# A hybrid decoder step on one core: TensorE in source order, gate and u products between the matmuls of S5 and attention

## The chip, the cores and the metric

The kernel runs on one core of one Trainium2 chip. The metric is the device time of one execution in microseconds. The kernel before takes 1735.41 us (median of 3 runs, 1729.68 to 1736.14).

## The reference

One layer of a hybrid decoder, for a prompt of 1024 tokens and for 8 sequences of 4 new tokens, of width 1024, all in float32:

```
proj = rmsnorm(x, norm1_g) @ w_in        # q, k, v (12 heads x 64), u (512), gate_a, gate_s (1024 each)
# branch A: for 3 dilation groups of 4 heads, causal dilated window attention with a bias by distance;
#           the groups of a head slot are merged by their softmax denominators -> 256 channels
# branch B: S5: 32 groups of 16 channels, each with a 64-wide complex diagonal state;
#           y = Re(C h) + D u, gelu, then y * sigmoid(y @ w_glu + b_glu)
mix = sigmoid(gate_a) * (attn_out @ w_branch_attn) + sigmoid(gate_s) * (ssm_out @ w_branch_ssm)
x   = x + mix @ w_out
a, val = split(rmsnorm(x, norm2_g) @ w_up)          # 2816 each
x   = x + (silu(causal_conv3(a)) * val) @ w_down    # then a final rmsnorm
```

It also returns the new key and value rows, the final S5 states and the convolution's last inputs. The samples attend to cached keys and values of up to 2048 positions.

## The kernel before, in words

All tokens form 1056 columns (4 residues of 256 prompt columns and 8 sample columns each); features lie on partitions. A matrix product is done in three fp32r passes (weights and activations each split into a high and a low part): `gemm` (L159) makes a tile of 128 outputs from 8 steps of k, each of 9 matmuls of 128x352. `load_w` (L145) fetches 128 columns of weights (two buffers), multiplies them by the norm's gain `g1c` where they meet x (L154), and splits them (L155, L156). Three PSUM banks hold one tile's result.

The work goes through stages:

- x is loaded, transposed and split raw (L226 to L243); 1/rms of each token is made beside it and spread over columns as `rb1`. Each product of x is multiplied by `rb1` when it leaves PSUM (L268 for u, L336 for gates, L732 for q, k, v), on VectorE.
- `u_tile` makes 4 tiles of u, which go to DRAM and come back in another layout as `U`. The bias table by distance is made by fp32 one-hot matmuls (L286).
- The parameters of S5 are worked out by a long chain of small operations on VectorE and POOL (L374 to L590), ending in the Toeplitz matrix `Mm`.
- The S5 loop (L605) takes 16 pairs of groups: two transpositions and two matmuls (L624), a rotation and scans on VectorE with one step on POOL (L631 to L644), copies of H on ScalarE (L646), three matmuls (L650 to L652) and a gelu.
- The attention takes 6 units (3 groups by 2 head pairs) of 8 blocks of queries. A block has logits (L839), the bias and row maxima on VectorE (L844), exp on ScalarE, transpositions to `pT`, a copy (L855) and the value product into `pO` (L858). Beside each block `cached` multiplies one sequence's cached keys by its queries on POOL (L817) and sums them on VectorE into `Lk` (L818). `proj` makes q, k, v of the next unit. `merge` combines the groups after each head pair; its weights are spread by transpositions of `lb` (L903).
- Then come the samples' attention (with V tiles loaded by POOL's queue, L967), the GLU and the projections of both branches, the output projection (L1102) and the channel mixer (L1147 on).

A planner orders every engine's instructions from its own estimate of their times, TensorE's too. `gates_after` binds 16 gate tiles to places named by `PLAN`: three after the S5 loop, six spread within it, two before units of the attention, and five after it. A gate tile gets its sigmoid (L337) and is stored in `sgd`.

Of the kernel before, what the change touches and what calls it, by code (L numbers as in the profile page):

```python
# [38 lines left out]
# columns of the one-hot matrix, group by group (dilation 1, 4, 16)  # L39
# [4 lines left out]
COFF = (R0W, R1W, R2W)                       # cached keys of the decode, in the group  # L44
SOFF = (R0W + 512, R1W + 128, R2W + 128)     # new keys of the decode, in the group
# [9 lines left out]
def _onehot():  # L55
    """[33, NCOLS]: column -> the bucket of its distance, or row 32 where the key is masked."""
# [26 lines left out]
    return (np.arange(33)[:, None] == idx[None]).astype(np.float32)  # L83
# [12 lines left out]
def body(tc, I, O):  # L96
# [12 lines left out]
    with root:  # L109
# [18 lines left out]
        rb1 = cst.tile([P, T], F32, name="rb1")  # L128
        prm = cst.tile([P, 2 * KD + 4], F32, name="prm")
        mult = cst.tile([P, 16], F32, name="mult")         # 0, 1, 2, ...  # L130
# [4 lines left out]
        cbf = cst.tile([P, NF, 16], F32, name="cbf")      # (i, b)  # L135
        g1c, g2c, bglu = prm[:, :KD], prm[:, KD:2 * KD], prm[:, 2 * KD:]

        nc.gpsimd.dma_start(g1c, I['norm1_g'][0].rearrange("(k p) -> p k", p=P), allow_slow_non_contiguous=True)
# [6 lines left out]
        def load_w(src, kt, g=None, mw=P, E1=V_, E2=V_):  # L145
            """mw columns of a weight matrix, [kt*128, mw] -> exact parts hi + lo, [128, kt, mw]."""
# [6 lines left out]
            if g is not None:  # L153
                E1.tensor_tensor(raw, raw, g[:, :kt, None].to_broadcast([P, kt, mw]), OP.mult)  # L154
# [4 lines left out]
        def gemm(ps, w, acts, m0=0, k0=0, by_chunk=False):  # L159
            """ps[c] += w^T act; acts: [(hi, lo)] by k."""  # L160
            hi, lo = w
            n = len(acts)
            if by_chunk:
                for c in range(NCH):
                    for k in range(n):
                        for j, (wt, xt) in enumerate(((lo, acts[k][0]), (hi, acts[k][1]), (hi, acts[k][0]))):
                            PE.matmul(ps[c][:, :CH], wt[:, k0 + k, m0:m0 + P], xt[:, cs(c)],
                                      start=k == 0 and j == 0, stop=k == n - 1 and j == 2)
                return
            for k in range(n):  # L170
# [4 lines left out]
                for c, j in runs:  # L175
                    wt, xt = ((lo, xh), (hi, xl), (hi, xh))[j]
                    PE.matmul(ps[c][:, :CH], wt[:, k0 + k, m0:m0 + P], xt[:, c * CH:(c + 1) * CH],  # L177
                              start=k == 0 and j == 0, stop=k == n - 1 and j == 2)

# [11 lines left out]
        xp_ = pool("xact", 1)  # L191
        xh = xp_.tile([P, KD, T], F32R, name="xh")
        xl = xp_.tile([P, KD, T], F32R, name="xl")
        X = [(xh[:, k], xl[:, k]) for k in range(KD)]
        xhv, xlv = (t.rearrange("p k (s c) -> p k s c", s=S4) for t in (xh, xl))

# [1 line left out]
        s2 = root.enter_context(ExitStack())  # L198
        sp = pool("s5", 1, stack=s2)

# [6 lines left out]
        st3 = xin.tile([P, 3, 9], F32, name="st3")  # L207
        st, rst, tmp12 = (st3[:, x] for x in range(3))
        G_.memset(st, 1.0)
# [11 lines left out]
        def x_tile(src, extra=False):  # L221
            t = go.tile([P, T], F32, name="go")[:, :D] if extra else xin.tile([P, D], F32, name="xt", bufs=4)
            nc.sync.dma_start(t[:src.shape[0]], src)
            return t[:src.shape[0]]

        xt0 = [x_tile(xpv[h][:, 0]) for h in range(2)]  # L226
        xs = x_tile(I['x_sample'].rearrange("b t d -> (b t) d"))
        for s in range(S4):
            xt = [x_tile(xpv[h][:, s], (s, h) in ((1, 1), (2, 0))) for h in range(2)] if s else xt0
            for k2 in range(0, KD, 2):  # L230
                pt = p3.tile([P, 512], F32, name="pt")
                for k in range(2):
                    for h in range(2):
                        tr(pt[:, (2 * k + h) * P:(2 * k + h + 1) * P], xt[h][:, (k2 + k) * P:(k2 + k + 1) * P])
                split(xhv[:, k2:k2 + 2, s, :256], xlv[:, k2:k2 + 2, s, :256], pt.rearrange("p (k c) -> p k c", k=2))
            if s == 0:
                pt = p3.tile([P, 512], F32, name="pt")
                for k in range(KD):
                    tr(pt[:, k * 32:(k + 1) * 32], xs[:, k * P:(k + 1) * P])
                split(xhv[:, :, :, 256:], xlv[:, :, :, 256:], pt[:, :256].rearrange("p (k b s) -> p k s b", k=KD, s=S4))  # L240
                A_.activation(xs, xs, AF.Square, accum_out=st[:32, 8:9])
            for h in range(2):
                A_.activation(xt[h], xt[h], AF.Square, accum_out=st[:, h * 4 + s:h * 4 + s + 1])  # L243
        rsqrt(rst, st, tmp12, V_)
        for s in range(S4):
            pt = p3.tile([P, 512], F32, name="pt")
            for h in range(2):
                tr(pt[:, h * P:(h + 1) * P], rst[:, h * 4 + s:h * 4 + s + 1].to_broadcast([P, P]))
            V_.tensor_copy(sc(rb1)[:, s, :256], pt[:, :256])
        pt = p3.tile([P, 512], F32, name="pt")  # L250
        tr(pt[:, :32], rst[:32, 8:9].to_broadcast([32, P]))
        V_.tensor_copy(sc(rb1)[:, :, 256:].rearrange("p s b -> p b s"), pt[:, :32].rearrange("p (b s) -> p b s", s=S4))
# [4 lines left out]
        sgd = dr.tile([2, D, T], F32, name="sgd")  # L257

# [1 line left out]
        udv = ud.rearrange("(i q) (s c) -> s q i c", q=32, s=S4)  # L260

        def u_tile(m):
            w = load_w(w_in[:, 2304 + m * P:2304 + (m + 1) * P], KD, g1c, E1=G_, E2=G_)
            ps = gbanks()
            gemm(ps, w, X, by_chunk=m == 0)
            uT = go.tile([P, T], F32, name="go")
            for c in range(NCH):
                V_.tensor_tensor(uT[:, cs(c)], ps[c][:, :CH], rb1[:, cs(c)], OP.mult)  # L268
            nc.sync.dma_start(ud[m * P:(m + 1) * P], uT)

        u_tile(0)

# [1 line left out]
        tab = xin.tile([33, 3, 32], F32, name="tab")  # L274
        G_.memset(tab, NEG)
        nc.gpsimd.dma_start(tab[:32, :, :4], I['rel_bias'].rearrange("b (g h) -> b g h", g=3))
        vec = dr.tile([4, NCOLS], F32, name="vec")
        blocks = [(g, a, min(512, GCOLS[g] - a)) for g in range(3) for a in range(0, GCOLS[g], 512)]
        for b0 in range(0, len(blocks), 4):
            pt = p3.tile([P, 512], F32, name="pt")  # L280
            for j, (g, a, n) in enumerate(blocks[b0:b0 + 4]):
                if j % 2 == 0:
                    oh2 = xin.tile([P, D], F32, name="xt", bufs=4)[:33]
                oh = oh2[:, j % 2 * 512:]
                nc.sync.dma_start(oh[:, :n], I['onehot'][:, GOFF[g] + a:GOFF[g] + a + n])
                PE.matmul(pt[32 * j:32 * j + 32, :n], tab[:, g], oh[:, :n], start=True, stop=True,  # L286
                          tile_position=(0, 32 * j))
# [1018 lines left out]
```

## Time and profile before

| what | value |
| --- | --- |
| median of 3 runs | 1735.41 us |
| profiled execution, span | 1739.8 us (no other time of it is shown) |
| busy PE / PEld / DVE / ACT / POOL | 95% / 89% / 50% / 28% / 27% of the span |
| instructions | 25386 |
| mean granted TensorE clock | 0.970 |
| bytes moved | 149.53 MB, mean 86 GB/s |

PE is TensorE's matmuls, PEld its weight loads, DVE VectorE, ACT ScalarE, POOL GpSimd, SP SyncE. PEclk is the granted TensorE clock, as a share of full speed. A busy PE includes matmuls that run at the low clock.

### The profile page before, as it was taken

How to read it: one execution, taken by the hardware profiler on the slowest of the kernel's cores; microseconds unless marked ns; L12 is line 12 of the kernel's file. 1: busy time of each engine (PE TensorE's matmuls, PEld its weight loads, DVE VectorE, ACT ScalarE, POOL GpSimd, SP SyncE). 2: the span in 40 equal slices, each digit the busy share in tenths (PEclk: the TensorE clock that was granted, in tenths of full speed). 3: DMA queues.
4: the chain of work that ended last, by engine and by line, in shares of the span. 5: the costliest groups of instructions: out<-in, count | busy, mean ns of one | idle time of the engine just before them, and what ended most of it. 6: DMA issues, size and time to landing. Idle time of an engine off the chain costs nothing.

```text
span 1739.8 us, 25386 instructions
## 1 busy us (share of the span) xinstructions
PE 1648.9 (95%) x10272; PEld 1554.8 (89%) x10272; DVE 865.4 (50%) x1472; ACT 495.2 (28%) x892; POOL 465.5 (27%) x498
## 2 busy tenths in 40 slices
PE   6978888988999999999999999999999999999997
PEld 5677778977888888979899999999999999999996
DVE  3598986344445544534763434434444344444445
ACT  5103333333433343421322222121121212111126
POOL 7474662022112202250672121020110201110114
PEclk9899999999999988999999999999999999999999
DMA  7341223254225413477711110211202111020122
GB/s 183 93 118 50 62 75 84 74 141 129 83 78 145 143 58 82 165 229 242 228 49 49 37 49 27 65 36 33 73 19 67 34 47 54 28 63 28 57 63 100
DMA packets 220094, 149.53 MB, mean 86 GB/s; under 512 B 30517, under 2 KB 208159, under 8 KB 219978
## 3 DMA queue, kind: packets, MB, share of 16 engines
q1 hardware_dynamic: 207002, 128.12, 25.3%
q10 hardware_dynamic: 10224, 10.36, 1.9%
q0 software_dynamic: 2752, 9.44, 1.6%
q8 instruction: 80, 1.31, 0.3%
q14 instruction: 36, 0.29, 0.1%
HBM read 122.03 MB, written 27.82 MB: 86 GB/s over the span
## 4 chain that ended last, share of the span: by engine, by line
PE 75%; DVE 10%; DMA 6%; issue 4%; POOL 3%; SPq 1%; ACT 1%; DVEq 0%; POOLq 0%; ACTq 0%
PE pg L177 68%; DMA qb<-qd 2%; DMA wraw<-in_w_in_dram 1%; PE pa L839 1%; DVE H L644 1%; PE pO L858 1%; PE pg L1250 1%; PE pT L142 1%; DVE mm L631 1%; PE pa L142 1%; POOL qb L817 1%; DVE wlo L156 1%; DVE wraw L154 1%; DVE mm L632 1%; DMA cache<-in_cache_kv_w_dram 1%
## 5 line engine op out<-in xcount | busy, mean ns | idle before, releaser
L177 PE MATMUL pg<-xh,wlo 128*128 128x352 f32 x1944 | 531.0, 332 | 24.5 <-DVE go L732 8.8
L177 PE MATMUL pg<-xl,whi 128*128 128x352 f32 x1944 | 526.7, 330 | 0.0
L177 PE MATMUL pg<-xh,whi 128*128 128x352 f32 x1944 | 526.2, 330 | 0.0
L177 PEld LDWEIGHTS pg<-xh,wlo 128*128 128x128 f32 x1944 | 354.0, 192 | 34.4 <-DVE go L732 9.9
L177 PEld LDWEIGHTS pg<-xl,whi 128*128 128x128 f32 x1944 | 355.0, 193 | 4.9 <-issue 3.9
L177 PEld LDWEIGHTS pg<-xh,whi 128*128 128x128 f32 x1944 | 354.2, 192 | 4.6 <-issue 3.5
L155 ACT CAST whi<-wraw 128x1024 fp32r<-128x1024 f32 (+2 forms) x156 | 132.9, 852 | 746.9 <-PE pg L177 478.2
L156 DVE TENSOR_TENSOR wlo<-wraw,whi 128x1024 fp32r<-128x1024 f32 (+2 forms) x152 | 158.0, 1039 | 65.2 <-ACT whi L155 63.4
L1153 POOL COPY ext<-ext 128x510 f32<-128x510 f32 x22 | 15.7, 712 | 524.5 <-DVE ext L1152 524.5
L177 PE MATMUL pg<-hh,wlo 128*128 128x352 f32 x480 | 148.0, 325 | 0.0
L177 PE MATMUL pg<-hl,whi 128*128 128x352 f32 x480 | 147.0, 322 | 0.0
L177 PE MATMUL pg<-hh,whi 128*128 128x352 f32 x480 | 146.6, 323 | 0.0
L817 POOL TENSOR_TENSOR qb<-kt,qb 128x512 f32<-128x512 f32 x48 | 62.1, 1304 | 277.6 <-DMA qb<-qd 219.9
L1180 DVE TENSOR_TENSOR y<-pg,y 128x352 f32<-128x352 f32 x168 | 84.6, 524 | 99.0 <-PE pg L177 98.3
L1152 DVE TENSOR_TENSOR ext<-pg,rb 128x352 f32<-128x352 f32 x66 | 32.7, 525 | 154.2 <-PE pg L177 154.2
L177 PEld LDWEIGHTS pg<-hh,wlo 128*128 128x128 f32 x480 | 88.9, 188 | 0.5
L177 PEld LDWEIGHTS pg<-hl,whi 128*128 128x128 f32 x480 | 89.2, 189 | 0.0
L177 PEld LDWEIGHTS pg<-hh,whi 128*128 128x128 f32 x480 | 88.7, 188 | 0.0
L1167 DVE TENSOR_TENSOR go<-pg,cv 128x352 f32<-128x352 f32 x66 | 31.2, 521 | 111.6 <-PE pg L177 111.6
L154 DVE TENSOR_TENSOR wraw<-wraw,prm 128x1024 f32<-128x1024 f32 x34 | 47.9, 1409 | 75.5 <-DMA wraw<-in_w_in_dram 75.5
L1161 POOL TENSOR_TENSOR cv<-cv,rb 128x1056 f32<-128x1056 f32 x22 | 54.3, 2469 | 55.0 <-ACT cv L1160 52.7
L818 DVE TENSOR_REDUCE Lk<-qb 128x8 f32<-128x512 f32 x48 | 33.0, 688 | 64.3 <-POOL qb L817 64.1
(585 smaller groups left out, 2301.7 us busy)
## 6 DMA issues: line engine op xcount, KB each, us to landing
wraw<-in_w_up_dram SPq DMA_DIRECT2D x44, 512.0 KB
wraw<-in_w_in_dram SPq DMA_DIRECT2D x38, 512.0 KB
qb<-qd SPq DMA_DIRECT2D x48, 256.0 KB
wraw<-in_w_down_dram SPq DMA_DIRECT2D x48, 192.0 KB
sgd<-go SPq DMA_DIRECT2D x16, 528.0 KB
kt<-in_cache_kv_w_dram SPq DMA_DIRECT2D x32, 256.0 KB
cache<-in_cache_kv_w_dram POOLq DMA_DIRECT2D x16, 512.0 KB, 5.7
go<-sgd SPq DMA_DIRECT2D x8, 528.0 KB
```

The source lines that it names most:

```text
L142: PE.transpose(out, in_, ident[:n, :n])
L154: E1.tensor_tensor(raw, raw, g[:, :kt, None].to_broadcast([P, kt, mw]), OP.mult)
L155: A_.copy(hi, raw)
L156: E2.tensor_tensor(lo, raw, hi.bitcast(F32), OP.subtract)
L177: PE.matmul(ps[c][:, :CH], wt[:, k0 + k, m0:m0 + P], xt[:, c * CH:(c + 1) * CH], start=k == 0 and j == 0, stop=k == n - 1 and j == 2)
L631: V_.tensor_tensor(m[x], ps[x][:, None, :256].to_broadcast([P, 2, 256]), rt, OP.mult)
L817: G_.tensor_tensor(qb, kv_, qb, OP.mult)
L818: V_.tensor_reduce(Lk[:, g, pr * 64:pr * 64 + 64].rearrange("p (h r) -> p h r", h=2)[:, :, 4 * b:4 * b + 4] .rearrange("p h t -> p t h"), ...
L1152: V_.tensor_tensor(ef[:, 2 * C + c * CH:2 * C + (c + 1) * CH], ps[c][:, :CH], rb2[:, cs(c)], OP.mult)
L1161: G_.tensor_tensor(cv, cv, rb2, OP.mult)
L1167: V_.tensor_tensor(t[:, cs(c)], ps[c][:, :CH], cv[:, cs(c)], OP.mult)
L1180: V_.tensor_tensor(y[m][:, cs(c)], ps[c][:, :CH], y[m][:, cs(c)], OP.add)
```

## The change

TensorE's instructions are taken in the order of the source up to the second merge, while the other engines stay with the planner. Products with `w_in` become jobs; `fill(n)` sets n steps of k of the next job at the place where it is called. Calls stand in the S5 preparation, in the S5 loop (8 gate tiles, 4 before it) and between the parts of every attention block (15 q, k, v tiles and 4 gates). The S5 loop makes the output of a pair one turn after its states, and the attention transposes and multiplies a block one turn after its logits. x is multiplied by 1/rms and by the gain, token by token, before it is transposed, so weights are no longer scaled and products are no longer multiplied by `rb1`; they leave PSUM by ScalarE. u is made in 16 pieces of 264 columns. x is read again and transposed for the residual. Sigmoids of the gates move to where the gates are read. The sums of cached products are issued behind the next block's maxima. The bias matmuls become fp32r with the table's high and low part on different partitions. Some loads move to ScalarE's queue. The diff, cut to its core:

```diff
-PLAN = (3, 6, 0, 0, 0, 0, 1, 1)
+PREP = 4
+LOOP = 8
...
-            if g is not None:
-                E1.tensor_tensor(raw, raw, g[:, :kt, None].to_broadcast([P, kt, mw]), OP.mult)
             A_.copy(hi, raw)
             E2.tensor_tensor(lo, raw, hi.bitcast(F32), OP.subtract)
...
+        front.enter_context(tc.manual_schedule(engines={mybir.EngineType.PE}))
+        def product(src, evac):
+            w = load_w(src, KD)
+            ps = gbanks()
+            yield from gemm_k(ps, w, X)
+            evac(ps)
+        def fill(n=None):
+            done = 0
+            while n is None or done < n:
+                if state["gen"] is None:
+                    if not jobs:
+                        return
+                    state["gen"] = product(*jobs.pop(0))
+                    state["left"] = KD
+                next(state["gen"])
+                done += 1
...
+        def normed(tiles, c0):
...
+            for j, (x, o) in enumerate(zip(tiles, out)):
+                A_.activation(o, x, AF.Square, accum_out=v[:, j:j + 1])
+            rsqrt(r, v, t, V_)
+            for j, (x, o) in enumerate(zip(tiles, out)):
+                V_.scalar_tensor_tensor(o, x, r[:, j:j + 1], g1b[:rows], OP.mult, OP.mult)
+        def u_part(s, m):
+            ps = banks[1].tile([P, 512], F32, name="pg")
+            r = slice(s * C, (s + 1) * C)
+            for k in range(KD):
+                for j, (wt, xt) in enumerate(((uw[m][1], X[k][0]), (uw[m][0], X[k][1]), (uw[m][0], X[k][0]))):
+                    PE.matmul(ps[:, :C], wt[:, k], xt[:, r], start=k == 0 and j == 0, stop=k == KD - 1 and j == 2)
+            uT = xin.tile([P, C], F32, name="uT", bufs=3)
+            A_.copy(uT, ps[:, :C])
+            nc.sync.dma_start(ud[m * P:(m + 1) * P, r], uT)
...
+                nc.scalar.dma_start(oh2[:, :n], I['onehot'][:, GOFF[g] + a:GOFF[g] + a + n])
...
+                G_.tensor_copy(ohr[:, :w2], oh2[:, :w2])
+                PE.matmul(pt[:, :n], tab[:, g, 96 - 32 * j:224 - 32 * j], ohr[:, j % 2 * 512:j % 2 * 512 + n],
...
             t = go.tile([P, T], F32, name="go")
             for c in range(NCH):
-                V_.tensor_tensor(t[:, cs(c)], ps[c][:, :CH], rb1[:, cs(c)], OP.mult)
-            A_.activation(t, t, AF.Sigmoid)
+                A_.copy(t[:, cs(c)], ps[c][:, :CH])
             nc.sync.dma_start(sgd[which, m * P:(m + 1) * P], t)
...
+        fill(4)
...
+        fill(KD * PREP - 8)
         G_.memset(Mm, 0.0)
         for i4 in range(4):
...
+            fill(2)
...
+        for i in range(NS + 1):
+            if i < NS:
+                states(i)
+            fill(1)
+            if i + 1 < NS:
+                em_of(i + 1)
+            fill(pending() - base * (NS - i) // (NS + 1) - 1)
+            if i:
+                y_of(i - 1)
+            fill(pending() - base * (NS - i) // (NS + 1))
+        fill()
...
+                def evac(ps):
+                    t = at.tile([P, T], F32, name="pt_")
+                    for c in range(NCH):
+                        A_.activation(t[:, cs(c)], ps[c][:, :CH], AF.Copy, scale=scale)
+                    o = at2.tile([P, 1024], F32, name=f"qkv{kind}", bufs=1 if kind == 2 else 2)
+                    V_.tensor_copy(grp_dst(o, g), grp(t, g))
...
+        def cached_sums(behind):
+            g, pr, b, qb = late.pop(0)
+            with tc.issue_after(behind.ins):
                 V_.tensor_reduce(Lk[:, g, pr * 64:pr * 64 + 64].rearrange("p (h r) -> p h r", h=2)[:, :, 4 * b:4 * b + 4]
                                  .rearrange("p h t -> p t h"), qb.rearrange("p t (h e) -> p t h e", e=HD), AX.X, OP.add)
...
+        def due(n):
+            return max(0, pending() - base * (NB8 - 1 - n) // NB8)
+        for n in range(NB8 + 1):
+            u, blk = divmod(n, 8)
+            if n < NB8:
...
+                pin = logits(sts[u], blk)
+                fill(min(1, due(n)))
             if n:
...
+                turned(sts[pu], pb)
+                fill(min(2, due(n)))
+                values(sts[pu], pb)
...
+            while len(late) > 1 or (late and n == NB8):
+                cached_sums(pin)
+            fill(due(n))
+        for _ in merge(1, ol[1]):
+            pass
         s3.close()
+        front.close()
...
+        for s in range(S4):
+            for h in range(2):
+                nc.sync.dma_start(xraw[2 * s + h][:, :D], xpv[h][:, s])
...
+                for k in range(2):
+                    A_.copy(xcol[k2 + k][:, s * C:s * C + 256], pt[:, 256 * k:256 * k + 256])
...
             nc.sync.dma_start(t, sgd[1, m * P:(m + 1) * P])
+            A_.activation(t, t, AF.Sigmoid)
...
-            G_.tensor_tensor(y[k], xh[:, k].bitcast(F32), xl[:, k].bitcast(F32), OP.add)
...
-                V_.tensor_tensor(y[m][:, cs(c)], ps[c][:, :CH], y[m][:, cs(c)], OP.add)
+                V_.tensor_tensor(y[m][:, cs(c)], ps[c][:, :CH], xcol[m][:, cs(c)], OP.add)
```

## Rows read from the trace of the kernel before

**Rows 1.** The page's strip of 40 slices: TensorE's busy tenths and granted clock.

```profile
PE   6978888988999999999999999999999999999997
PEclk9899999999999988999999999999999999999999
```

**Rows 2.** Windows: stretch, width, busy (count) PE PEld DVE ACT POOL, clock, DMA share, GB/s.

```profile
0.00:143.00 143.00, 115.21 (x823) 96.63 (x824) 89.39 (x141) 38.58 (x62) 82.89 (x124) 0.92 0.45 121
143.00:293.00 150.00, 126.03 (x654) 112.14 (x653) 130.09 (x186) 51.90 (x150) 91.72 (x85) 0.94 0.20 60
293.00:348.00 55.00, 55.00 (x349) 54.98 (x348) 20.42 (x27) 17.37 (x17) 0.00 (x0) 1.00 0.38 105
348.00:690.00 342.00, 317.66 (x2009) 279.52 (x2007) 153.99 (x427) 128.78 (x320) 69.75 (x58) 0.93 0.40 109
690.00:856.00 166.00, 161.19 (x1050) 146.01 (x1047) 79.77 (x117) 46.93 (x65) 54.06 (x52) 0.99 0.65 216
```

**Rows 3.** Windows, one slice of the attention.

```profile
652.50:696.00 43.50, 41.49 (x253) 35.77 (x254) 18.16 (x58) 16.67 (x38) 12.49 (x12) 0.82 0.31 82
```

**Rows 4.** Waits of VectorE in the attention: total us, times, longest us.

```profile
DVE Lk L818 <- POOL qb L817: 64.1, 37, 5.7
DVE wraw L154 <- DMA wraw<-in_w_in_dram: 44.9, 16, 5.8
```

**Rows 5.** Waits of TensorE in the attention.

```profile
PE pa L839 <- DVE md L844: 12.6, 6, 5.4
```

**Rows 6.** Waits in the S5 loop.

```profile
ACT fin L646 <- DVE H L643: 58.8, 15, 5.4
PE pa L651 <- ACT H L647: 12.2, 9, 2.9
```

**Rows 7.** Chain of waits in order of time: start, us, what, count.

```profile
1309.95 365.71 PE pg L177 x2268
...
1696.87 3.49 PE pg L142 x32
1700.37 2.79 PE pg L1250 x12
```

**Rows 8.** Groups of TensorE by shape, whole span: count, busy us, mean ns.

```profile
L286 PE MATMUL pt<-xt,tab 33*32 33x512 f32 x26 | 10.0, 905 | 0.1
```

**Rows 9.** Timeline of TensorE at the front: start, us, operation.

```profile
4.89 0.87 PE L142 MATMUL pt<-ident,xt 128*128 128x128 f32 x3 [4.89 <-DMA xt<-in_x_prompt_dram]
```

**Rows 10.** Timeline of ScalarE at the front.

```profile
37.47 1.06 ACT L243 ACTIVATE xt<-xt 128x1024 f32<-128x1024 f32 x1
```

**Rows 11.** Timeline of VectorE at the front: first and last step of 1/rms.

```profile
42.43 0.16 DVE L213 TENSOR_SCALAR st<-st 128x9 f32<-128x9 f32 x1
...
44.03 0.17 DVE L219 TENSOR_TENSOR st<-st 128x9 f32<-128x9 f32 x1
```

**Rows 12.** Groups of VectorE by shape, 130 to 290 us.

```profile
L156 DVE TENSOR_TENSOR wlo<-wraw,whi 128x1024 fp32r<-128x1024 f32 x7 | 11.5, 1644 | 0.0
L154 DVE TENSOR_TENSOR wraw<-wraw,prm 128x1024 f32<-128x1024 f32 x7 | 10.1, 1438 | 4.0 <-DMA wraw<-in_w_in_dram 4.0
L336 DVE TENSOR_TENSOR go<-pg,rb 128x352 f32<-128x352 f32 x20 | 9.7, 513 | 0.1
```

**Rows 13.** Groups of TensorE in the S5 loop, one of three alike.

```profile
L177 PE MATMUL pg<-xl,whi 128*128 128x352 f32 x151 | 45.8, 353 | 0.0
```

**Rows 14.** Groups of ScalarE by shape, 690 to 860 us.

```profile
L1050 ACT ACTIVATE go<-pg,prm 128x352 f32<-128x352 f32 x12 | 6.4, 554 | 18.2 <-PE pg L177 18.0
```

**Rows 15.** Groups of VectorE by shape, 690 to 860 us.

```profile
L336 DVE TENSOR_TENSOR go<-pg,rb 128x352 f32<-128x352 f32 x12 | 5.8, 521 | 6.7 <-PE pg L177 6.6
```

**Rows 16.** Timeline of TensorE in the second merge: first and last of six.

```profile
692.14 0.60 PE L142 MATMUL pa<-ident,lb 128*128 128x128 f32 x4
...
705.77 0.60 PE L142 MATMUL pa<-ident,lb 128*128 128x128 f32 x4
```

**Rows 17.** DMA of 690 to 860 us, strip of 40 slices: GB/s.

```profile
GB/s 0 4 157 94 279 370 367 56 251 0 4 211 39 18 317 219 350 226 254 229 282 365 351 297 154 168 248 343 146 260 230 188 351 192 264 263 327 292 257 249
```

More of the change, by code (lines that the diff above doesn't have):

```diff
@@ L82, in _onehot @@
     assert idx.shape == (NCOLS,)
-    return (np.arange(33)[:, None] == idx[None]).astype(np.float32)
+    hot = np.zeros((97, NCOLS), np.float32)
+    for r in (0, 64):
+        hot[r:r + 33] = np.arange(33)[:, None] == idx[None]
+    return hot
 def V(ap, off, dims):
@@ L157, in load_w, with gemm, gemm_k @@
             return hi, lo
-        def gemm(ps, w, acts, m0=0, k0=0, by_chunk=False):
+        def gemm(ps, w, acts, m0=0, k0=0):
+            for _ in gemm_k(ps, w, acts, m0, k0):
+                pass
+        def gemm_k(ps, w, acts, m0=0, k0=0):
             hi, lo = w
             n = len(acts)
[L163 to L169, printed above, removed]
             for k in range(n):
@@ L219, in rsqrt, with x_tile @@
             E.tensor_tensor(r, r, t, OP.mult)
-        def x_tile(src, extra=False):
-            t = go.tile([P, T], F32, name="go")[:, :D] if extra else xin.tile([P, D], F32, name="xt", bufs=4)
+        def x_tile(src):
+            t = xin.tile([P, D], F32, name="xt", bufs=7)
             nc.sync.dma_start(t[:src.shape[0]], src)
             return t[:src.shape[0]]
[L226 to L252, printed above, removed]
         w_in = I['w_in'][0]
@@ new lines, in normed @@
+        def normed(tiles, c0):
+            n = len(tiles)
+            rows = tiles[0].shape[0]
+            v, r, t = (st3[:rows, x, c0:c0 + n] for x in range(3))
+            out = [xin.tile([P, D], F32, name="xn", bufs=3)[:rows] for _ in tiles]
+            for j, (x, o) in enumerate(zip(tiles, out)):
[3 more added lines that the diff above has]
+                V_.scalar_tensor_tensor(o, x, r[:, j:j + 1], g1b[:rows], OP.mult, OP.mult)
+            return out
@@ new lines, in turn_x @@
+        def turn_x(s, xt):
+            xn = normed(xt, 2 * s)
+            for k2 in range(0, KD, 2):
+                pt = p3.tile([P, 512], F32, name="pt")
+                for k in range(2):
+                    for h in range(2):
+                        tr(pt[:, (2 * k + h) * P:(2 * k + h + 1) * P], xn[h][:, (k2 + k) * P:(k2 + k + 1) * P])
+                split(scx(xh[k2 // 2])[:, :, s, :256], scx(xl[k2 // 2])[:, :, s, :256], pt.rearrange("p (k c) -> p k c", k=2))
+        def u_part(s, m):
[7 more added lines that the diff above has]
+            nc.sync.dma_start(ud[m * P:(m + 1) * P, r], uT)
@@ new lines, in body @@
+        xts = [[x_tile(xpv[h][:, 0]) for h in range(2)]]
+        xs = x_tile(I['x_sample'].rearrange("b t d -> (b t) d"))
+        u_weights(0)
+        for s in range(1, S4):
+            xts.append([x_tile(xpv[h][:, s]) for h in range(2)])
+            u_weights(s)
+        turn_x(0, xts[0])
+        xsn = normed([xs], 8)[0]
+        pt = p3.tile([P, 512], F32, name="pt")
+        for k in range(KD):
+            tr(pt[:, k * 32:(k + 1) * 32], xsn[:, k * P:(k + 1) * P])
+        for k2 in range(4):
+            split(scx(xh[k2])[:, :, :, 256:], scx(xl[k2])[:, :, :, 256:],
+                  pt[:, k2 * 64:k2 * 64 + 64].rearrange("p (k b s) -> p k s b", k=2, s=S4))
@@ new lines, in body @@
+        SM = sp.tile([P, 24, NS], F32, name="SM")
+        V_.tensor_copy(SM[:, 0:4], pt[:, 0:64].rearrange("p (a i) -> p a i", a=4))
+        u_part(0, 2)
+        u_part(0, 3)
+        turn_x(2, xts[2])
+        for m in range(4):
+            u_part(1, m)
+        turn_x(3, xts[3])
+        for m in range(4):
+            u_part(2, m)
+        tabf = xin.tile([P, D], F32, name="xt", bufs=7)[:97, :672].rearrange("p (g c) -> p g c", g=3)
+        tab = xin.tile([97, 3, 224], F32R, name="tab")
@@ L678, in body @@
                                   fo[NB * i4:NB * i4 + NB])
-        for _ in range(PLAN[0]):
-            gate(*gates.pop(0))
-        gates_after(pins, PLAN[1])
         s2.close()
@@ L771, in attn, with unit_keys @@
                 A_.copy(KV[:, b4 * 4:b4 * 4 + 4, 1], pt.rearrange("p (b f) -> p b f", b=4))
+            hs = slice(pr * P, (pr + 1) * P)
+            pt = pa.tile([P, 512], F32, name="pa")
+            for kind in range(3):
+                tr(pt[:32, kind * P:(kind + 1) * P], smf[kind][:, g, pr])
+            V_.tensor_copy(SMP[:, g, :, hs], pt[:32, P:3 * P].rearrange("p (k f) -> p k f", k=2))
+            qs_ = dk.tile([32, P], F32, name="qs_", bufs=1)
+            V_.tensor_copy(qs_, pt[:32, :P])
+            nc.sync.dma_start(qd[:, g, hs], qs_)
+            return KV
+        def unit_keys(g, pr, k, KV):
+            hs = slice(pr * P, (pr + 1) * P)
             kout = ((7,), (1, 3, 5, 7), tuple(range(8)))[g]
@@ new lines, in cached @@
+        def cached(g, pr, b):
+            kt = dk.tile([P, 4, P], F32, name="kt", bufs=3)
+            src = caches[g][b, :, 0, 2 * pr:2 * pr + 2].rearrange("n h e -> n (h e)")
+            if g == 0:
+                nc.sync.dma_start(kt[:, 0], src)
+                kv_ = kt[:, None, 0].to_broadcast([P, 4, P])
+            else:
+                nc.sync.dma_start(kt, src.rearrange("(n r) f -> n r f", r=DIL[g])[:, :4])
+                kv_ = kt
+            qb = dk.tile([P, 4, P], F32, name="qb", bufs=3)
+            nc.sync.dma_start(qb, V(qd, b * 4 * 768 + g * 256 + pr * P, [[0, P], [768, 4], [1, P]]))
+            G_.tensor_tensor(qb, kv_, qb, OP.mult)
+            late.append((g, pr, b, qb))
@@ new lines, in logits @@
+        def logits(st, blk):
+            g, bt = st["g"], st["bt"]
+            q, k = st["qkv"][:2]
+            if blk % 2 == 0:
+                st["pS"] = [pa.tile([P, 512], F32, name="pa") for _ in range(2)]
+                for x in range(2):
+                    ck = chunks_of(g, blk + x)
+                    for h in range(2):
+                        r = slice(64 * h, 64 * h + 64)
+                        PE.matmul(st["pS"][h][:, x * 256:x * 256 + len(ck) * P], q[r, (blk + x) * P:(blk + x + 1) * P],
+                                  k[r, ck[0] * P:(ck[-1] + 1) * P], start=True, stop=True)
+            n = len(chunks_of(g, blk))
+            W = n * P
+            bo = 0 if g == 2 or n == 2 else P
+            so = blk % 2 * 256
+            s_ = at2.tile([P, 512], F32, name="s_")
+            md = st["md"]
+            for h in range(2):
+                V_.tensor_tensor_reduce(s_[:, h * W:(h + 1) * W], st["pS"][h][:, so:so + W],
+                                        bt[:, h, bo:bo + W], 1.0, -3e38, OP.add, OP.max, md[:, blk, h:h + 1])
+            nm = at2.tile([P, 2], F32, name="nm")
+            pin = V_.tensor_scalar(nm, md[:, blk, 0:2], -1.0, None, OP.mult)
+            for h in range(2):
+                A_.activation(s_[:, h * W:(h + 1) * W], s_[:, h * W:(h + 1) * W], AF.Exp, bias=nm[:, h:h + 1],
+                              accum_out=md[:, blk, 2 + h:3 + h])
+            st["s"][blk] = s_
+            return pin
@@ new lines, in turned, with values @@
+        def turned(st, blk):
+            s_ = st["s"].pop(blk)
+            n = len(chunks_of(st["g"], blk))
+            pT = pa.tile([P, 512], F32, name="pT", bufs=1)
+            for j in range(2 * n):
+                tr(pT[:, j * P:(j + 1) * P], s_[:, j * P:(j + 1) * P])
+            pTs = at2.tile([P, 512], F32, name="pTs")
+            A_.copy(pTs[:, :2 * n * P], pT[:, :2 * n * P])
+            st["pTs"][blk] = pTs
+        def values(st, blk):
+            g, pr, og = st["g"], st["pr"], st["og"]
+            pTs = st["pTs"].pop(blk)
+            chunks = chunks_of(g, blk)
+            n = len(chunks)
+            b4, b = blk // 4, blk % 4
+            if b == 0:
+                st["pO"] = pa.tile([P, 512], F32, name="pO", bufs=1)
+            pO = st["pO"]
+            for j, kb in enumerate(chunks):
+                for h in range(2):
+                    PE.matmul(pO[64 * h:64 * h + 64, b * P:(b + 1) * P], st["KV"][:, kb, 1, 64 * h:64 * h + 64],
+                              pTs[:, (h * n + j) * P:(h * n + j + 1) * P], start=j == 0, stop=j == n - 1)
+            cached(g, pr, blk)
+            if b == 3:
@@ L948, in body @@
-        gates_after([pin], len(gates))
+        qkvs = [[] for _ in units]
+        bts = {0: bias_tile(*units[0])}
+        jobs += proj(*units[0], qkvs[0])
+        fill()
+        rest = gates[PREP + LOOP:]
+        for n in range(1, len(units)):
+            jobs += proj(*units[n], qkvs[n])
+            if n < len(units) - 1 and len(rest) > 3:
+                jobs.append(rest.pop(0))
+        jobs += rest
+        NB8 = 8 * len(units)
+        base = pending()
+        sts, ol, merging, late = {}, [{}, {}], None, []
@@ L1076, in body @@
         keep.close()
+        rb1 = pool("rbp", 1).tile([P, T], F32, name="rb1")
         psum(8)
```

357 lines of the change are left out of this document (178 added, 179 removed).

## The prediction

> **What bounds the kernel now.** I first read the strip of 40 slices [rows 1]. The reader is to see that PE stands at 6 to 8 in most of the first ten slices and at 9 from the eleventh to the last but one, and that PEclk falls to 8 in slices 2, 15 and 16. A 9 says only "90% or more", so the strip places the loss early and can't size it. Next I cut the span into stages: front and S5 preparation (1), S5 loop (2), a stretch of products alone (3), prompt attention (4), samples and branch projections (5) [rows 2], and from 856 us on the output projection and the mixer (6). TensorE is idle for 27.8, 24.0, 0, 24.3 and 4.8 us in stages 1 to 5, together 80.9 us. The granted clock there is 0.92, 0.94, 1.00, 0.93 and 0.99 of full speed; one minus it, times the stage, is 11.4 + 9.0 + 0 + 23.9 + 1.7 = 46.0 us. Idle time inside a low-clock stretch counts twice in this, so the loss lies between 81 and 127 us. I take 127: in one slice of the attention PE was busy for 41.49 of 43.50 us at a clock of 0.82 [rows 3], so the low clock hits matmuls, not gaps. TensorE's work up to the output projection is then 856 − 127 = 729 us.
>
> What it waits for I read from the waits of each stage. In the attention, VectorE stands at the head of its queue for 64.1 us for cached products and for 44.9 us for weights that it has to scale [rows 4], and the row maxima, on which TensorE's next logits wait, are queued behind. TensorE's own row for that is 12.6 us in 6 waits [rows 5]. In the S5 loop VectorE is busy for 130.1 of 150 us [rows 2] and TensorE waits 12.2 us for H [rows 6].
>
> **The change, part by part.** Prices of TensorE work come from the chain of waits [rows 7]: 2268 product matmuls take 365.7 us, 0.161 us each, so a tile of 72 is 11.6 us and one step of k (9 matmuls) 1.45 us. A transposition is two records; 32 records take 3.49 us, so it is 0.22 us.
>
> *Work added and removed on TensorE.* Re-reading x for the residual adds 64 full transpositions and 8 of the samples, 72 × 0.22 = +15.7 us, in stage 5. The bias product goes from 13 fp32 matmuls of 512 columns, 10.0 us [rows 8], to 13 in fp32r; 12 such of 512 columns take 2.79 us [rows 7], so 3.0 us: −7 us. The u product becomes 384 matmuls of 264 columns in place of 288 of 352. No row shows 264 columns in fp32r. The line through 352 and 512 columns (0.161 and 0.233) gives 0.121 us, 46.4 us in all, as before; if the pitch stays at 0.161 it is +15.4 us; at the 0.109 of a record of a transposition it is −4.5. I take 0, since that record shows a matmul with a weight load of its own passing in less than 0.121. TensorE's work becomes 729 + 15.7 − 7 = 738 us. The other products and matmuls stay the same in number.
>
> *Stage 1.* x is now normalised first. For the first two tiles that is two squares of 1.06 us, the small chain to 1/rms (from 42.43 to 44.20 us) and two products of 1024 columns (1.44 us, as the scaling of a weight) [rows 10 to 12], about 7 us: the first transposition moves from 4.9 [rows 9] to 12 us. After that pieces of u stand ready between the transpositions, and 28 steps of gates (41 us) ahead of the Toeplitz matmuls cover the chain of small S5 operations, while VectorE no longer scales weights; TensorE's own work is then later than that chain. I allow 9 us of waits, 21 in all, against 39 lost now.
>
> *Stage 2.* Some 60 steps of gates (87 us) are spread over 17 turns. S5's own matmuls: 126 us busy, less 3 × 151 products at 0.161 (73 us) and 9 us of low clock, leave 44 [rows 2, 13], so TensorE needs 131 us. VectorE has 130 us, loses 10.1 of scaling and 9.7 of evacuation and gains one weight split of 1.64: 112 us [rows 2, 12]. TensorE becomes the bound by 19 us. The evacuations go to ScalarE, 3 × 0.554 us a tile [rows 14]; its idle time hides them unless its order puts them behind H (rival A). I allow 11 us against 33.
>
> *Stages 3 and 4.* The three products alone stay at full speed. In the attention the scaling and its waits are gone, and the sums of the cached products are put one block later, behind the next block's maxima: of the 64.1 us that VectorE stood still, little is left ahead of logits [rows 4]. The added wait holds the sum and what follows it on VectorE by at most one maximum; Lk is read after the attention. The copies of q, k, v go from ScalarE to VectorE and three evacuations a tile from VectorE to ScalarE; both engines are idle for over half the stage [rows 2]. Each of 48 blocks has about 3.2 steps (4.6 us) of product between its own matmuls, over twice the mean wait behind a maximum (12.6/6 = 2.1), though less than the longest, 5.4 [rows 5]. I allow 0.3 us a block, 14 us, against 48 lost now.
>
> *Stage 5.* Here the change takes cover away. Now four gate tiles (12 evacuations [rows 15]), 46 us, run beside the merge and the samples; afterwards none is left. The last block, the round trip of its maxima and the second merge are then bare: in that merge the transpositions run from 692.1 to 706.4 [rows 16], so I take 16 us, and 3 for the low clock behind it. Samples and GLU can fill each other; 10 us more. That is 29 us against 6.5 lost now. ScalarE gains 64 copies at some 0.5 us and the sigmoids (8 at some 1.1, 24 at 0.55), about 54 us on the 46.9 of 166 that it has [rows 2, 14]: hidden, with some 101 of 158 us. Without that room the x columns would be late only for the output projection.
>
> *Queues and the rest.* The sigmoids leave the loop; POOL loses eight sums in the output projection, beside PE without a gap: 0 us. The one-hot rows (97 in place of 33), the S5 scalars and the g1 row go from SP's and POOL's queues to ScalarE's, some 18 issues, where ScalarE is busy for 38.6 of 143 us [rows 2]: 0 us. The x tiles (4.3 MB) join SP's queue in stage 5 while four stores of gate tiles (2.2 MB) leave it: the stage's 36 MB (216 GB/s for 166 us [rows 2]) become 38.
>
> **The sum.** Loss after: 21 + 11 + 0 + 14 + 29 = 75 us. The output projection starts at 738 + 75 = 813 in place of 856, 43 us earlier; stage 6 keeps its 884 us. The span goes from 1739.8 to 1697. The profiled execution shows no time of its own beside its span, which lies 4.4 us above the median of the three runs (1735.41); with the same distance the time is **1692 us**, 2.5% less.
>
> That VectorE and ScalarE are strict queues, while TensorE may take weight loads ahead, is stated by the Trainium skill (TensorE: Matmul & The Clock Gate, the section on the array and its engine queue depths). The trace agrees: the 64.1 us for sums whose data were not there held the maxima behind them [rows 4]. By that rule alone the move of the evacuations to ScalarE speaks against the change: it is rival A's, at 1714.
>
> **The rivals.**
>
> A. *ScalarE holds the evacuations in the S5 loop.* It waits 58.8 us in 15 waits for H there, 3.9 each [rows 6]. If the evacuations of each of the 8 tiles fall behind one, TensorE, with three banks, stands: 8 × 3.9 = 31 us, and 2, in place of 11, so +22: 1714. For it: the H copies have to be in that queue at every turn. Against: TensorE's work per turn is now longer than VectorE's, so H comes early.
>
> B. *Stage 5 becomes bound by its transfers.* 38 MB at the stage's present 216 GB/s are 176 us [rows 2]; I forecast 159.5 − 46 + 15.7 + 29 = 158 for it: +18, 1710. For it: 24 V tiles and nine x tiles are wanted at once. Against: slices of that stretch reach 370 GB/s [rows 17].
>
> C. *The fixed order itself is the bound.* A matmul set in source order holds all behind it when its operand is late. At the mean wait behind a maximum, 2.1 us [rows 5], in each of 48 blocks it costs 101 us where I count 14: +87, **1779**, slower. It decides from 0.3 + 43/48 = 1.2 us a block. For it: what gave TensorE other work was the planner's freedom. Against: a block's transpositions come a turn after its logits, and VectorE is half empty.
>
> D. *Nearly all waits go.* 15 + 5 + 0 + 5 + 15 = 40 us lost in place of 75: 1657. For it: stage 3 shows 55 us without a gap where products alone are wanted. Against: stage 5 has no cover.
>
> That the change does not do what it says has no room: the order is written out.
>
> **Chances.** Forecast 0.45 (own range 1675 to 1705), A 0.10, B 0.12, C 0.15, D 0.18. To hold 8 in 10 I reach down to 1652, D with the u pieces at their cheapest, and up to 1738, which takes A and B with the u pieces at +15 and the mild end of C; left out are the lower part of D (0.08) and most of C (0.11). Within 0.5%, about what a measurement of this kernel can tell from no change (1726.7 to 1744.1), I put the mild end of C and the upper ends of A and B, 0.07; slower 0.11; faster 0.82.
>
> **What would show it.** In the slices: PE at 9 from about slice 2 on with a dip near slice 16 (the merge), PEclk at 9 throughout the attention. The first transposition near 12 us; an S5 loop of about 142 us with VectorE busy for near 112; an output projection that starts near 813. VectorE's waits for cached products and for weights gone or small, TensorE's for maxima under 15 us. Rival A shows as TensorE waiting for ScalarE's copies of products in the loop, B as TensorE waiting for cache, sgd or msd tiles, C as idle time before logits or values in most blocks. The forecast is wrong if the output projection starts later than 845 or earlier than 780.

## The result and the profile after

The change made the kernel slower: 1780.35 us (median of 4 runs, 1776.33 to 1783.3) against 1734.34 us before; ratio 1.0269, 95% interval 1.0244 to 1.0295. I had forecast 1692. The profiled execution of the changed kernel took 1776.33 us, with a span of 1774.5.

The page's strips (TensorE's busy tenths, the granted clock, the rate of all transfers), which answer to [rows 1]:

```profile
PE   3256899899999999698899999999999999999997
PEclk9678899999999999899999999999999999999999
GB/s 199 44 42 119 104 50 73 61 115 89 152 107 114 146 133 102 208 199 188 246 106 40 45 48 33 39 60 24 73 26 65 35 32 72 23 66 23 60 62 99
```

From slice 6 on the picture is what the forecast asked for: 9 nearly throughout, and the clock at 9 through the attention. In slices 2 to 4 TensorE is busy for 2 to 6 tenths, and in two of them the transfers run at 42 to 44 GB/s.

The windows by stage (columns as in [rows 2]; stages 1 to 5):

```profile
0.00:242.00 242.00, 143.33 (x1108) 137.20 (x1109) 82.05 (x162) 50.55 (x98) 74.84 (x126) 0.84 0.34 98
242.00:383.00 141.00, 129.28 (x715) 120.67 (x714) 110.52 (x158) 39.64 (x156) 89.02 (x85) 0.96 0.21 65
383.00:421.00 38.00, 37.43 (x235) 36.73 (x234) 7.88 (x11) 7.77 (x15) 0.00 (x0) 1.00 0.39 111
421.00:731.00 310.00, 304.82 (x2095) 274.02 (x2096) 126.04 (x379) 125.29 (x344) 72.20 (x56) 1.00 0.49 130
731.00:889.00 158.00, 134.13 (x855) 117.00 (x852) 68.72 (x117) 57.98 (x108) 51.20 (x51) 0.89 0.65 212
```

TensorE is idle for 98.7, 11.7, 0.6, 5.2 and 23.9 us in them. I had allowed losses of 21, 11, 0, 14 and 29, but these also held the time lost to the low clock, so the two are not the same measure. The lengths compare better: stage 2 took 141 us against 142 forecast, stage 5 158 against 158, and the attention is idle for less than its allowance. The output projection starts at 890.2 us in place of 813, 77 us late, and this lateness comes from stage 1, where TensorE is idle for 98.7 us.

The waits of TensorE in stage 1, and under them those of ScalarE from 24 to 150 us ("issue" is time in which an engine waited for nothing that the profile shows):

```profile
PE pt L144 <- DVE xl L186: 50.6, 4, 19.5
PE pt L144 <- DVE xn L292: 17.3, 1, 17.3
PE pg L310 <- ACT xh L185: 9.2, 3, 7.7
PE pa L144 <- DMA ctok<-in_state_ssm_re_dram: 8.6, 1, 8.6
```

```profile
ACT uT L312 <- issue: 47.2, 3, 23.8
ACT xh L185 <- issue: 24.6, 2, 13.4
```

TensorE waits for the low part of x, which waits for the cast of the high part on ScalarE, and ScalarE waits for nothing visible. ScalarE's own timeline with its issues (ACTq) shows what it does:

```profile
29.22 0.47 ACTq L384 DMA_DIRECT2D xt<-in_onehot_dram  x1
29.74 1.86 ACTq L387 DMA_DIRECT2D xt<-in_onehot_dram  x1
31.69 7.79 ACTq L384 DMA_DIRECT2D xt<-in_onehot_dram  x1
39.52 0.21 ACT L185 CAST xh<-pt 128x64 fp32r<-128x64 f32 x1 [11.28 <-issue]
39.57 8.63 ACTq L387 DMA_DIRECT2D xt<-in_onehot_dram  x1
```

The issue of most one-hot loads lasts 5 to 9 us, and the cast stands behind it. Of the 13 issues, from 29 to 121 us, the two short ones at the start, a later one of 0.2 us and ten of 5.4 to 8.6 us come to 76 us. In the kernel before, the 13 issues with 33 rows stood on SyncE's queue (shortest, median, longest in ns): all but one took 0.3 us.

```profile
L285 SPq DMA_DIRECT2D xt<-in_onehot_dram x13: 289/298/1997, 23.3 to 54.3; - x13
```

The transfers of 60 to 72 us, for most of which nothing else runs (queue, kind: packets, MB, share of 16 engines):

```profile
q10 hardware_dynamic: 142, 0.29, 6.2%
```

q10 is ScalarE's queue. 6.2% is one engine of 16, and 0.29 MB in 12 us are 24 GB/s; a load of 198 KB then needs 8 us.

### The profile page after: what moved, and what is told of

It is laid out like the page before. It is cut to its first block, busy times and chain, and to the rows that moved or that the text cites. A ratio compares the mean times of both kernels' runs of the same rounds, so it can differ in the third digit from the quotient of the medians.

```text
span 1774.5 us, 25821 instructions
## 1 busy us (share of the span) xinstructions
PE 1624.3 (92%) x10418; PEld 1553.0 (88%) x10418; DVE 782.1 (44%) x1405; ACT 498.0 (28%) x1009; POOL 433.6 (24%) x492
## 4 chain that ended last, share of the span: by engine, by line
PE 76%; DMA 7%; DVE 6%; ACTq 3%; issue 3%; ACT 2%; POOL 1%; SPq 1%; DVEq 0%; POOLq 0%
PE pg L174 67%; ACTq L384 2%; DMA xt<-in_onehot_dram 1%; PE pa L144 1%; DMA go<-sgd 1%; DVE H L732 1%; PE pa L946 1%; PE pO L986 1%; PE pg L310 1%; ACTq L387 1%; PE pg L1449 1%; DMA msd<-go 1%; DVE mm L719 1%; DVE wlo L156 1%; POOL n L728 1%
## 5 line engine op out<-in xcount | busy, mean ns | idle before, releaser
L174 PE MATMUL pg<-xh,wlo 128*128 128x352 f32 x1872 | 489.4, 335 | 12.4 <-ACT go L441 10.5
L174 PE MATMUL pg<-xh,whi 128*128 128x352 f32 x1872 | 470.4, 324 | 0.0
L174 PE MATMUL pg<-xl,whi 128*128 128x352 f32 x1872 | 469.1, 324 | 0.0
L174 PEld LDWEIGHTS pg<-xh,wlo 128*128 128x128 f32 x1872 | 328.8, 190 | 28.4 <-ACT go L441 13.2
L174 PEld LDWEIGHTS pg<-xl,whi 128*128 128x128 f32 x1872 | 332.5, 190 | 0.2
L174 PEld LDWEIGHTS pg<-xh,whi 128*128 128x128 f32 x1872 | 332.1, 189 | 0.0
L156 DVE TENSOR_TENSOR wlo<-wraw,whi 128x1024 fp32r<-128x1024 f32 (+2 forms) x154 | 163.3, 1060 | 104.9 <-ACT whi L155 102.7
L144 PE MATMUL pt<-ident,xn 128*128 128x128 f32 (+1 forms) x72 | 12.7, 336 | 68.6 <-DVE xl L186 50.6
L144 PEld LDWEIGHTS pt<-ident,xn 128*128 128x128 f32 (+1 forms) x72 | 10.2, 179 | 70.0 <-DVE xl L186 51.7
```

Source lines behind the costliest of these rows:

```text
L144: PE.transpose(out, in_, ident[:n, :n])
L156: E2.tensor_tensor(lo, raw, hi.bitcast(F32), OP.subtract)
```

## The experiments

Theory A: 97 rows are not shared out over the DMA engines, so that each load takes one engine for 8 us, and the issuing queue stands. Theory B: issuing from ScalarE is the cost, whatever the rows. Theory C: TensorE's written order waits for other things. Times are medians, ratios are to the kernel before, which was measured again beside each group of runs and had 1729.8 to 1730.8 us.

**112 rows, from ScalarE's queue.**

```diff
-    hot = np.zeros((97, NCOLS), np.float32)
+    hot = np.zeros((112, NCOLS), np.float32)
```

> The changed kernel with the one-hot array padded with zero rows from 97 to 112 (7 x 16) and loaded so, still from ScalarE's queue; the matmuls read 97 rows as before. Theory A (a load of 97 rows goes through one DMA engine at 25 GB/s, 198 KB in 7.8 us, and the next loads on ScalarE's queue hold ScalarE meanwhile, 76 us in all): the 13 loads take about 1 us each, ScalarE is not held, the S5 loop starts at 155 to 170 us in place of 242, time 1695 to 1712 us. Theory B (issuing transfers from ScalarE's queue is the cost, whatever their rows): 1780 us as before. Theory C (TensorE's fixed order in stage 1 waits on other things): the loads get short but the loop starts after 225 us, time above 1760 us.

1719.4 us (ratio to before 0.993, interval 0.9904 to 0.9956). Fifteen rows of zeros take some 60 us off the changed kernel. The issues last 0.3 to 0.45 us, the loop starts at 181.7 us in place of 241.8, and from 30 to 36 us ScalarE's queue has a share equal to ten engines:

```profile
q10 hardware_dynamic: 560, 1.02, 65.6%
```

B is out. The loop still starts later than A's 155 to 170, and the time is above A's 1712; TensorE's waits in stage 1 are now:

```profile
PE pt L144 <- DVE xn L292: 17.4, 1, 17.4
PE pa L144 <- DMA ctok<-in_state_ssm_re_dram: 8.7, 1, 8.7
PE pt L144 <- DVE xl L186: 5.5, 4, 3.6
PE pt L144 <- issue: 4.5, 1, 4.5
PE pt L144 <- DVE go L397: 3.5, 1, 3.5
```

**97 rows, from SyncE's queue.**

```diff
-                    nc.scalar.dma_start(oh2[:, :n], ...)
+                    nc.sync.dma_start(oh2[:, :n], ...)
```

> The changed kernel with the 13 loads of 97 rows issued from SyncE's queue in place of ScalarE's. The loads still take 7.8 us each, 101 us in all. If what hurts is that ScalarE is held (theory A): its casts run on time, the loop starts at 155 to 175 us, time 1695 to 1715 us. If what hurts is that TensorE's order waits for the late one-hot rows (theory C with the loads as the late thing): the first one-hot matmul stands at 60 us or later and the last near 135 to 150 us, the loop starts after 220 us, 1760 to 1780 us.

1785.3 us (1.031, 1.0279 to 1.0341). No gain; my reading that ScalarE would be free once the issues leave its queue was wrong. The loop starts at 246.8 us. The one-hot matmuls all run between 143 and 155 us, so they are late, as C has it, but the time lies above C's range too. The issues last as long on SyncE, and from 46 to 56 us, when the loads have its queue to themselves, its share is again that of one engine:

```profile
29.47 0.29 SPq L384 DMA_DIRECT2D xt<-in_onehot_dram  x1
29.81 2.63 SPq L387 DMA_DIRECT2D xt<-in_onehot_dram  x1
32.55 7.59 SPq L384 DMA_DIRECT2D xt<-in_onehot_dram  x1
```

```profile
q1 hardware_dynamic: 126, 0.26, 6.6%
```

TensorE still waits 54.0 us in four waits for the low part of x. All x tiles had been issued by 26 us; what SyncE holds back now are a load of weights and the stores of u. ScalarE's copies into the three buffers `uT` wait for these stores, and its casts stand behind the copies:

```profile
ACT uT L312 <- DMA ud<-uT: 77.5, 4, 38.1
```

So the harm reaches ScalarE by another way, through buffers that come free late.

**96 rows and one row.**

```diff
-                    nc.scalar.dma_start(oh2[:, :n], I['onehot'][:, ...])
+                    for r0, r1 in ((0, 96), (96, 97)):
+                        nc.scalar.dma_start(oh2[r0:r1, :n], I['onehot'][r0:r1, ...])
```

> The changed kernel with each one-hot load issued as two from ScalarE's queue: rows 0 to 95 and row 96 alone; the same array, the same bytes, 26 issues in place of 13. Theory A (97 is no multiple of 16, so the rows are not shared out over the 16 DMA engines): the part of 96 rows takes about 1 us, the loop starts at 155 to 175 us, 1695 to 1715 us, as with 112 rows. Theory B (the number of issues on ScalarE's queue): at or above 1780 us.

1722.2 us (0.9948, 0.9924 to 0.9971), above A's range as with 112 rows: the same bytes in twice the issues, and the loss is gone. On this queue it is neither the bytes nor the number of issues, but the row count of a load.

**The kernel before with 97-row loads from ScalarE's queue, and with 112.**

```diff
-                nc.sync.dma_start(oh[:, :n], I['onehot'][...])
+                nc.scalar.dma_start(oh[:, :n], I['onehot'][...])
```

(with an array of 97, or 112, rows)

> The kernel before with only the one-hot loads of the change: 97 rows (the last 64 zero) in place of 33, from ScalarE's queue in place of SyncE's; the matmuls read 33 rows. Theory A: ScalarE is held for some 70 us of stage 1, in which it has 39 us of work, the S5 loop starts 30 to 80 us later, 1765 to 1815 us. Theory C (only TensorE's written order makes the loads hurt; here the order is the planner's): 1734 us within 9.

> The kernel before with one-hot loads of 112 rows (33 used, the others zero) from ScalarE's queue in place of 33 from SyncE's: the same as the run with 97 rows but for 15 rows of zeros more. Theory A (the row count alone costs): 1731 us within 9, as the kernel before. Theory B (ScalarE's queue costs too): above 1750 us.

97 rows: 1813.2 us (1.0479, 1.044 to 1.0519); 112 rows: 1731.8 us (1.0009, 0.9989 to 1.0028). So this one part, put into the kernel before, costs 82 us without any written order, and nothing with 112 rows. In the first of the two TensorE waits for the loads and ScalarE stands behind its issues:

```profile
PE pt L288 <- DMA xt<-in_onehot_dram: 31.0, 7, 6.5
ACT L467 <- issue: 36.8, 1, 36.8
```

**98 rows, and 106.** The same edit as for 112.

> The changed kernel with 98 rows (2 x 7 x 7) in place of 97 (a prime), from ScalarE's queue. If rows are shared out by the largest divisor up to 16 (here 14, as 11 would be for the 33 rows of the kernel before): loads near 1 us, DMA rates far over 25 GB/s, 1716 to 1726 us as with 112. If only a multiple of 16 is shared out: 25 GB/s and 1780 us. If by the common divisor with 16 (2): 50 GB/s, 3.9 us a load, some 1740 us.

> The changed kernel with 106 rows (2 x 53), from ScalarE's queue. Largest divisor up to 16 is 2: two engines, near 50 GB/s, some 4.2 us a load, 55 us in all; time between the 1719 of 112 rows and the 1780 of 97, 1730 to 1755 us. If only a prime number of rows were slow: 1719 us.

98 rows: 1718.8 us (0.993, 0.9906 to 0.9954), as 112. 106 rows: 1735.1 us (1.002, 1.0001 to 1.004), between the two, with long issues of 2.5 to 5.5 us. ScalarE's queue with 98 rows (30 to 36 us) and with 106 (33 to 43 us):

```profile
q10 hardware_dynamic: 480, 0.87, 52.2%
```

```profile
q10 hardware_dynamic: 230, 0.46, 12.0%
```

12.0% is two engines of 16, at 23 GB/s each. The five counts fit one rule: a load takes as many engines as the largest divisor of its rows up to 16, that is 1 for 97, 2 for 106, 14 for 98, 16 for 112 and 96. The share shows the engine count directly for 97 and 106 only; 98, 112 and 96 (46.7% from 30 to 36 us) show that it was not small. The Trainium skill states this rule (DMA: Bandwidth & Descriptors, the section on why a DMA increments its semaphore by 16 and not by 1) and gives 127 partitions as a case of one engine; these runs agree.

**97 rows, from GpSimd's queue.**

```diff
-                    nc.scalar.dma_start(oh2[:, :n], ...)
+                    nc.gpsimd.dma_start(oh2[:, :n], ...)
```

> The changed kernel with the 13 loads of 97 rows issued from GpSimd's queue (1780 us from ScalarE's, 1785 from SyncE's). If the harm is the queue that stands still behind a slow load, the casts on ScalarE and the x tiles on SyncE run on time here, and GpSimd's own work (the casts of the one-hot rows and the S5 preparation) is held in their place: if its queue stands as the others did, 1755 to 1790 us; if it takes issues without standing, 1720 to 1745 us, with the one-hot matmuls as the late thing. If the loads of this queue are shared out over the DMA engines in another way: 1715 to 1725 us.

1710.9 us (0.9884, 0.9851 to 0.9916), 8 us below 112 rows from ScalarE and below all that I gave; the loop starts at 174.5 us, and what brings these last us was not separated. An issue costs GpSimd 0.6 us, and from 30 to 36 us its queue has 62% of 16 engines:

```profile
30.00 0.56 POOL L387 DMA_DIRECT2D xt<-in_onehot_dram  x1
```

```profile
q0 software_dynamic: 416, 1.04, 62.2%
```

So the rule holds on ScalarE's queue, and for 97 rows on SyncE's (both marked hardware in the rows), and not on this one.

**What else stage 1 loses.** Three steps on top of 112 rows.

```diff
+        fill(8)          # behind the last u piece
...
-        fill(KD * PREP - 8)
+        fill(KD * PREP - 16)
```

> The changed kernel with the one-hot rows padded to 112, and eight steps of the first gate product set in TensorE's order right after the last u piece, ahead of the transpositions of the convolution's parameters (the later call for 24 steps becomes 16). With 112 rows alone TensorE was busy for 10.0 of the 20 us from 100 on, where those transpositions wait for their loads. If these waits are what stage 1 still loses: 8 to 14 us less than the 1719 us with 112 rows alone, 1705 to 1712. Rival: the gate's weights are late as well, as their load stands on SyncE's queue behind the transfers that wait for the bias rows: 1719 within 4, the hole then sits ahead of the gate.

1713.8 us (0.991, 0.9894 to 0.9927): 5.6 us by the medians, less than I asked of it; by the ratios it is 3.5 us, and their intervals overlap. The wait for the S5 states stays, 9.6 us. Then:

```diff
-        for h in range(4): nc.sync.dma_start(z2[h], ...), z1, z0     # behind the bias rows
+        ... the same behind the loads of U
-            h0t = bp.tile([P, 4, 2, 64], F32, name=f"ctok{x}")...    # in the S5 preparation
+            h0t = xin.tile([P, D], F32, name="xt", bufs=7)...        # ahead of it
```

> As the run with eight gate steps set earlier, and the twelve copies z<-vec issued behind the loads of U, and the two loads of the old S5 states taken into buffers of the x pool ahead of the prep (TensorE waited 8.7 us for them). If SyncE's queue, held by transfers that wait for the bias rows, is what makes loads late in stage 1: another 8 to 15 us, 1692 to 1706. If it is not: as without it.

1701.3 us (0.9839, 0.9824 to 0.9853), another 12.5 us: the wait for the states is gone and the loop starts at 161.7 us. The two edits were not tried apart. And:

```diff
-        for _ in merge(1, ol[1]):
-            pass
+        for _ in merge(1, ol[1]):
+            fill(1)          # 8 steps kept out of the attention
```

> As the run with the copies issued later, and the last gate product (8 steps, 10.6 us) kept out of the attention and set between the steps of the last merge, where TensorE waits bare for some 16 us. If the attention is bound by TensorE's work (busy for 306 of 310 us): 7 to 13 us less than without it. If it is bound by its chains: no gain.

1717.9 us (0.9931, 0.9914 to 0.9949): 16.6 us slower than without it, a miss. The attention lost time although it had 10.6 us less to do: its last value product starts at 667.1 us in place of 653.8. The windows of 455 to 555 us, first without, then with the edit:

```profile
455.00:555.00 100.00, 97.91 (x670) 87.83 (x671) 39.80 (x134) 39.90 (x115) 22.84 (x18) 1.00 0.50 125
```

```profile
455.00:555.00 100.00, 89.35 (x592) 79.60 (x592) 38.95 (x124) 36.98 (x108) 23.13 (x18) 0.97 0.47 120
```

TensorE's waits for the copies of turned probabilities went from 3.4 us in 5 to 14.8 us in 14:

```profile
PE pO L987 <- ACT pTs L973: 14.8, 14, 2.8
```

The steps between the blocks are the cover; where they are missing the chain of a block comes out, which is what rival C warned of. What I overlooked is where they went missing. A unit's q, k, v must be complete before its first block, and `while len(qkvs[u]) < 3: fill(1)` sets what is left of them in one run. At the slower pace that is 8 steps ahead of four of the units (from 493.4 to 509.2 us, for instance, where TensorE has products alone), and the next blocks then get no steps: their value products at 511.3, 515.6 and 520.4 us all wait for the copies. Without the edit such a run was at most 5 steps long. So the run shows what uneven cover costs, more than what 8 steps fewer cost.

**All of it together**: 97 rows from GpSimd's queue, the steps set earlier, the copies later.

> The edits of the run with gate steps set earlier and copies z<-vec issued later (1701 us with 112 rows from ScalarE's queue), with 97 rows from GpSimd's queue in place of 112 from ScalarE's. If the 8 us that GpSimd's queue gained over 112 rows (1711 against 1719) come from other waits than those which the other edits took away: 1691 to 1697 us. If from the same: 1699 to 1704 us.

1693.8 us (0.978, 0.9753 to 0.9806), the fastest of all. Its stage 1 ends near 156.5 us (stages 1 and 5):

```profile
0.00:156.70 156.70, 132.57 (x1108) 126.98 (x1109) 87.96 (x162) 51.06 (x98) 80.48 (x139) 0.96 0.54 151
...
648.00:805.00 157.00, 135.52 (x856) 117.75 (x856) 69.30 (x118) 58.42 (x110) 52.38 (x52) 0.90 0.64 210
```

## Why the prediction was wrong

**The step that failed** is the one under queues: the one-hot rows "(97 in place of 33)" go to ScalarE's queue, "0 us". I counted 18 issues against ScalarE's idle time and gave neither an issue's length nor the new row count a price, though I named it. With 97 rows each load runs on one engine and ten of the 13 issues hold ScalarE for 5 to 9 us each. That term measures some 60 us by the padded run, and 82 us when put into the kernel before.

**The losses left in stage 1** were mis-sized. With 112 rows TensorE is idle for 43.3 us of the 181.7 (busy for 138.4), against the 21 that I allowed for idle time and low clock together:

```profile
0.00:181.70 181.70, 138.39 (x1106) 132.54 (x1107) 82.28 (x162) 51.25 (x98) 74.57 (x126) 0.92 0.48 132
```

The first transposition comes at 17.3 us, not 12. Transfers that wait for the bias rows stand ahead of the states and the gate weights on SyncE's queue. The run with gate steps set earlier and the one that moved the copies and the loads of the states took 18 us off together. I had looked at what leaves and joins the queues, not at what stands in them behind a wait.

**Work on TensorE.** The one price that no row of before showed, 264 columns in fp32r, was taken as 0.121 us. The chain of waits (start, us, what, count) gives 2.90/24 = 0.121 for an unbroken piece of u:

```profile
137.50 2.90 PE pg L310 x24
```

**Stage 2** took 141 us against the 142 that I named, with VectorE busy for 110.5 against 112. TensorE's wait for ScalarE's copies of products, the mark of rival A, is there, but small beside the 31 us that A would need; it answers to [rows 6]:

```profile
PE pg L174 <- ACT go L441: 10.5, 7, 3.7
```

**Stages 3 and 4** came out a little better than forecast: TensorE idles for 5.2 us in the attention where 14 were allowed. VectorE's wait for cached products fell from 64.1 us [rows 4] to 12.4, and TensorE's for maxima from 12.6 us [rows 5] to 0.4:

```profile
DVE Lk L933 <- POOL qb L927: 12.4, 5, 3.3
```

```profile
PE pa L144 <- DVE md L955: 0.4, 1, 0.4
```

Rival C is not what happened here: its 1779 us, so near the measured 1780, is a coincidence, as it put the idle time into the attention. The run with the last gate moved out shows how near C is all the same.

**Stage 5** took 158 us, as forecast, with 23.9 us idle against the 29 allowed, and 212 GB/s; rival B did not appear. Its granted clock was 0.89 all the same, so the length agrees better than the split into idle and low clock. Stage 6 took 884.3 us against the 884 of before. The output projection starts at 890.2 us, beyond the 845 from which I called the forecast wrong.

**The last step of the sum** missed too. The span came out 77 us above the 1697 that I forecast, the time 88 above 1692. I took the median to lie 4.4 us below the span, as before; here it lies 5.9 us above it (1780.35 against 1774.5). One profiled execution was no measure of that distance, and 10 us of the miss come from it.

So the mechanism of the change was read rightly in four of five stages; with 112 rows it comes to 1719 us, and with the loads on GpSimd's queue, gate steps set earlier and the copies later, to 1694. That the last lies 2 us from the forecast is no merit of it: that kernel has edits which I did not forecast.

## What to carry to other kernels

A changed row count can change a load's speed, as it did here on ScalarE's and SyncE's queues: look at the divisors of the rows, and at the share of the queue in the transfers' view (6.2% is one engine). An issue can hold the engine that makes it, so loads are counted in the time their issues take, not in their number. And when a step is moved, read what stands on its queue behind a waiting transfer.

## What the hardware showed that I had not expected

- A 198 KB load of 97 rows ran at 24 GB/s on one engine of 16, with 98 rows on over half of them; 106 rows used two.
- An issue on ScalarE's or SyncE's queue, otherwise 0.3 us, lasted 4 to 10 us with such loads under way, from the third load on, and all work of that engine stood behind it. How many loads a queue takes before it stands was not measured.
- From GpSimd's queue the same 97 rows were shared out (62% of 16 engines).
- TensorE's granted clock fell to 0.53 in the thin stretch from 57 to 72 us, in which it was busy for 5.6 of 15 us, so most of that stretch ran at the lower of its two levels:

```profile
57.00:72.00 15.00, 5.58 (x29) 5.22 (x30) 4.71 (x17) 4.89 (x11) 2.28 (x10) 0.53 0.12 43
```
